# Reordering loads, conversions and gate operations at the start and in the second sweep of a hybrid GLA/MLA layer

## Chip, cores and metric

The kernel runs on one core of one Trainium2 chip, as one program. The time is the device time of one execution in microseconds; a smaller time is better. Times of several executions are given as their median.

## The reference

One layer of an encoder on 2048 tokens of width 1024, float32. The input projection feeds two groups of heads: gated linear attention (GLA) in chunks, forward and backward, with a low-rank gate; and multi-head latent attention (MLA) with rotary keys and a softmax over all keys. Both outputs pass one output projection, a residual and a layer norm.

```python
h = x @ w_in                      # columns: q k v gate lr_f lr_b | cq ckv kr gate
log_a = log_sigmoid(lr @ wg2 + bg) / 16            # decay, per direction
o_a = rms_norm(gla(q, k, v, log_a_fwd) + flip(gla(flip(q, k, v, log_a_bwd)))) * silu(gate)
q = rms_norm(cq) @ w_uq;  kv = rms_norm(ckv) @ w_ukv
o_b = softmax(q_nope k_nope^T + rope(q_rope) rope(k_rope)^T) v * silu(m_gate)
out = layer_norm(alpha * x + concat(o_a, o_b) @ w_out)
```

## The kernel before, in words

Float32 operands are split into a high part (a copy to fp32r, helper `hi`, line 367, mostly on ScalarE, ACT) and a low part (the difference, helper `lo`, line 373, on VectorE, DVE, or GpSimd, POOL). A product is then three matmuls, high by high, high by low and low by high (`mm3`, lines 421 to 423). Because helpers record these operations, the profile's lines are told apart by the names of the tiles. The 2048 tokens are 16 chunks of 128.

**First sweep** (`sweep_a`): step i handles chunk 15 - i. `products` multiplies the chunk's x (`xah`, `xal`) by the GLA weights `wA` in three groups of columns (288, 384, 384), eight products of 128 rows each, into PSUM tiles `ipa`. What a group yields is then taken out: `lr` (the low-rank gate input) and `q2` from group 0, `k2` and `v1` from group 1, `v3` from group 2. `ga_lrT` transposes lr (tile `lrT`) and copies it to `lrTs`; `ga_z` multiplies it with the gate weights `wg` (matmul z, line 891); three ACT functions, VectorE's running sums and so on follow. Before step 0 stands a prologue: the loads of x for chunk 15 (`xaf`), of 13 weight pieces (`was0` to `was2`, in `W_PIECES`), the identity, the gate weights `wgf` with a column `wgm`, and the next x; every piece is converted to `wah` and `wal` in a chained order (`in_order(worder)`). Loads are issued on SyncE's queue (SP). Steps 0 to 3 are interleaved by the list `ORDER_A`, which fixes the order on every engine; elsewhere a scheduler in the framework orders the instructions of each engine by their place in the program and by when their inputs are ready. A closed pool's space is reused tile by tile.

**Between the sweeps** (`late_gates`): the weights `wm` and `wz` of the second sweep are converted by `load_ws` from pools of 17 buffers for 8 raw pieces, 8 high and 8 low parts. The order of ACT and VectorE there is fixed by the lists `TAIL_ACT` and `TAIL_DVE`.

**Second sweep** (`sweep_c`): eight steps of two chunks. Each small operation has a name and a place: step number plus a number from `PLACE_C` (or `PLACE_C_FIRST` for step 0 and `PLACE_C_LAST` for step 7; the two numbers of a pair are for the even and the odd chunk). All operations are sorted by place and written in that order, chained on every engine:

```python
last = dict(self.tail)
for _, _, fn, a in sorted(todo, key=lambda e: e[:2]):
    with self.in_order(last):
        fn(*a)
```

The names that matter here: `xh`, `xl` are the high and low part of a chunk's x, in the tiles `xch` (ACT) and `xcl` (POOL), which hold one step's two chunks; `ipa` to `ipd` are the four quarters of the chunk's product with `wm` (tile `ipm`, line 1281, six matmuls each); `pz` 0 to 7 are the eighths of the step's product with `wz` (line 1210); `gm1` to `gm4` make the MLA gate from it (ACT, ACT, ACT, VectorE; lines 1215 to 1224); `qhb`, `qlb`, `MMh`, `MMl` prepare the operands of `Ob`, the output of the GLA state (lines 1438 and 1439); `oia`, `oib`, `rgd`, `og` turn that into the normed output (VectorE, og at line 1465); `krf` and `krfa` apply the rotary angles to the key (VectorE, then an addition on POOL, line 1315); `tm` transposes; `pq` is the absorbed query product. `Ob`, the gate product `pz` and `pq` share a PSUM pool `gp` of two buffers. In a step after the first, the matmuls of a chunk's quarters stand in this order, with x's low part as the third kind:

```python
order = [(p, k) for k in range(NK) for p in range(2)] + [(2, k) for k in range(NK)]
x = (self.xch, self.xch, self.xcl)[p]
```

So quarter `ipc` reads the first two pieces of `xcl` and `ipd` the other six. `pz` n reads all of both chunks' x of two of the eight pieces in step 7, pieces 2n and 2n + 1 for n up to 3. After the second sweep come the softmax attention and the output projection, which the change leaves alone.

Of the kernel before, what the change touches and what calls it, by code (L numbers as in the profile page):

```python
# [9 lines left out]
F32 = mybir.dt.float32  # L10
F32R = mybir.dt.float32r
I32 = mybir.dt.int32
AF = mybir.ActivationFunctionType
ALU = mybir.AluOpType
# [4 lines left out]
P = 128  # L19
S = 2048  # L20
D = 1024
NK = D // P
NCH = S // P
H = 4
# [116 lines left out]
    Ob=(0.141, 0.861),  # L141
# [50 lines left out]
    gm2=0.832,  # L192
# [66 lines left out]
    MMl=(-0.109, 0.558),  # L259
    krfa=(-0.119, 0.94),  # L260
    krsl=(0.252, 1.09),
# [9 lines left out]
    gm1=0.643,  # L271
    gm2=0.686,
    gm3=0.706,
    gm4=0.804,
    sgm=1.056,
# [10 lines left out]
    ipd=(0.042, 0.445),  # L286
    Ob=(-0.03, 0.299),
    tm=(0.495, 1.083),
# [30 lines left out]
    qrTl=(1.081, 2.186),  # L319
    xl=(-0.244, 0.038),  # L320
    M=(-0.531, -0.11),
# [35 lines left out]
class K:  # L357
# [100 lines left out]

    def load_ws(self, pool, srcs, ncols, tag, on_pool=()):


        names = lambda p: [f"{tag}{p}{k}" for k in range(NK)]
        raw = [pool.tile([P, ncols], F32, tag=tag, name=n) for n in names("r")]
        for r, src in zip(raw, srcs):
            self.w_load = self.nc.sync.dma_start(r, src).ins
        yield
        wh = [pool.tile([P, ncols], F32R, tag=tag, name=n) for n in names("h")]
        W = []
        for k, n in enumerate(names("l")):
            wl = pool.tile([P, ncols], F32R, tag=tag, name=n)  # L470
            self.hi(wh[k], raw[k])
            self.lo(wl, raw[k], wh[k], "pool" if k in on_pool else "dve")
            W.append((wh[k], wl))
        yield W

# [140 lines left out]
    def sweep_a(self):  # L616
        tc, nc, ins, cp = self.tc, self.nc, self.ins, self.cp
        with ExitStack() as ctx:
# [6 lines left out]
            rmask = wp.tile([P, H, P], F32, name="rmask")  # L625
            wgm = wp.tile([98, 1], F32, name="wgm")
            wg = wp.tile([98, H, P], F32R, name="wg")
# [17 lines left out]
            with tc.tile_pool(name="sta", bufs=1, reuse_waits="tile") as sta:  # L645
                xf = self.load_x(NCH - 1, "xa", 1, 2)
                xcur = self.split_x(xp, xf, NCH - 1, "xa", "dve", 2)
                wgf = sta.tile([98, H * P], F32, name="wgf")
                wgh = sta.tile([98, H * P], F32R, name="wgh")
                wdone, worder = [], {}  # L650
                for g, (c0, n) in enumerate(A_GROUPS):
                    k = 0
                    for m in W_PIECES[g]:
                        st = sta.tile([P, m, n], F32, name=f"was{g}_{k}")
                        nc.sync.dma_start(st, ins[f"wA{g}"][:, k:k + m])
                        ks, cs = slice(k, k + m), slice(c0, c0 + n)
                        with self.in_order(worder):
                            for e in [slice(j, j + 1) for j in range(m)] if g == 0 else [slice(0, m)]:
                                kh, kl = wah[:, ks, cs][:, e], wal[:, ks, cs][:, e]
                                ops = self.hi(kh, st[:, e]), self.lo(kl, st[:, e], kh)  # L660
                        k += m
                        wdone.append(ops)
                    if g == 1:
                        nc.sync.dma_start(self.ident, ins["ident"])
                        nc.sync.dma_start(wgf, ins["wg"])
                        nc.sync.dma_start(wgm, ins["wgm"])
                with self.in_order(worder):
                    self.hi(wgh, wgf)
                    nc.vector.scalar_tensor_tensor(wg.rearrange("p h d -> p (h d)"), wgh.bitcast(F32), wgm[:, 0:1],
                                                   wgf, ALU.mult, ALU.add)  # L670
                xnext = self.split_x(xp, self.load_x(NCH - 2, "xa", 1, 2), NCH - 2, "xa", "dve", 2)
                nc.sync.dma_start(rmask, ins["rmask"])
                nc.sync.dma_start(mask, ins["mask"])
# [8 lines left out]
            run = lambda n, i: [0 for _ in getattr(self, "ga_" + n)(ch[i])]  # L682
            ch[0]["x"], ch[1]["x"] = xcur, xnext

# [14 lines left out]
            self.first_lr = wdone[7][0]  # L699
            step(0, {(1, 7): [("lrT", "cur")]})  # L700
            run("bst", 0)
# [42 lines left out]
    def products(self, d, g, after=lambda g, k: None):  # L744
# [16 lines left out]
        if i == 0 or i > 3:  # L761
            for n in (("lr", "q2"), ("k2", "v1"), ("v3",))[g]:
                for _ in getattr(self, "ga_" + n)(d):
                    pass
# [303 lines left out]
    def late_gates(self):  # L1068
# [7 lines left out]
        self.wabs_l = bc.tile([P, 2, H, P], F32R, name="wabs_l")  # L1076
        wm = self.load_ws(self.wm, [ins["wB"][k, :, 512:960] for k in range(NK)], 448, "wm")
        wz = self.load_ws(self.wz, [ins["wB"][k, :, 960:1472] for k in range(NK)], 512, "wz")
        next(wm)
# [887 lines left out]
def layouts(inputs):  # L1967
# [19 lines left out]
    wg, bg = wg.reshape(32, H * P), bg.reshape(1, H * P)  # L1987
    a["wg"] = np.concatenate([wg, wg, wg, bg, bg], axis=0)
    wgm = np.zeros((98, 1), np.float32)
    wgm[64:96] = -1.0  # L1990
    wgm[97] = -1.0
    a["wgm"] = wgm
    a["gn_col"] = g["gla_norm_g"][0].reshape(P, 1)
# [41 lines left out]
```

## Time and profile before

| | us |
|---|---|
| median of 3 executions | 1308.29 (1307.52 to 1310.21) |
| the profiled execution | 1306.76 |
| its span, first to last instruction | 1304.7 |
| TensorE busy | 1284.8 (98%) |
| VectorE, ScalarE, GpSimd busy | 961.9, 817.2, 785.9 |

The first sweep with its prologue takes the first 360 us or so of the span, the second sweep runs to about 612, the attention and the output projection fill the rest. In the page's chain of work that ended last, TensorE has 91%. A row of the timeline gives start and duration in us, engine, line, operation, output tile, input tiles, shapes and, in brackets, how long the engine sat idle before it and what ended that. Ends of matmuls are modelled; the distance between two starts is the better measure of their rate.

### The profile page before, as it was taken

The numbers are of one execution on the slowest core, as the hardware profiler recorded it, in microseconds if no ns is written. First come the engines' busy times: TensorE is split into PE (matmuls) and PEld (weight loads), VectorE is DVE, ScalarE is ACT, GpSimd is POOL, SyncE is SP. The second block draws the span as 40 slices with busy tenths as digits, with TensorE's granted clock in tenths as the row PEclk, the third lists the DMA queues.
The fourth block names the chain that finished last, engine by engine and source line by source line (L and its number), as shares of the span: only waits on it lengthen the run. The fifth ranks groups of instructions, "written<-read, shape, count | busy, mean of one in ns | idle before, by whom it ended". The sixth has DMA issues, their size and how long they took to land.

```text
span 1304.7 us, 19969 instructions
## 1 busy us (share of the span) xinstructions
PE 1284.8 (98%) x7082; PEld 1131.1 (87%) x7082; DVE 961.9 (74%) x1706; ACT 817.2 (63%) x1334; POOL 785.9 (60%) x494
## 2 busy tenths in 40 slices
PE   7999999999999999999999999999999999999997
PEld 7999999999999999999788888888888887888886
DVE  6966675656675555555888888888888888469997
ACT  6765655566676566564778787878888888511110
POOL 0143333242467667661488888889999999844441
PEclk9999999999999999999999999999999999999999
DMA  8132313131475555656301111121123210366662
GB/s 285 62 101 54 94 53 94 49 88 59 155 247 194 187 178 200 207 176 209 90 1 41 41 42 41 41 62 60 57 71 101 47 41 9 121 203 202 214 196 97
DMA packets 105908, 145.81 MB, mean 112 GB/s; under 512 B 16743, under 2 KB 59375, under 8 KB 105809
## 3 DMA queue, kind: packets, MB, share of 16 engines
q1 hardware_dynamic: 97744, 142.41, 34.8%
q0 software_dynamic: 672, 2.10, 0.4%
q8 instruction: 56, 0.92, 0.3%
q10 hardware_dynamic: 7392, 0.03, 0.3%
q14 instruction: 44, 0.35, 0.1%
HBM read 94.14 MB, written 50.36 MB: 111 GB/s over the span
## 4 chain that ended last, share of the span: by engine, by line
PE 91%; DVE 2%; ACT 2%; issue 1%; POOL 0%; SPq 0%; DMA 0%; DVEq 0%; ACTq 0%
PE pz L1210 7%; PE ipm L1281 5%; PE o L421 5%; PE o L423 5%; PE o L422 5%; PE pS L1541 4%; PE pS L1544 4%; PE pS L1543 4%; PE pS L1545 4%; PE pS L1542 4%; PE ipa L421 4%; PE ipa L422 4%; PE ipa L423 4%; PE po L421 2%; PE po L423 2%; PE po L422 2%
## 5 line engine op out<-in xcount | busy, mean ns | idle before, releaser
L373 POOL TENSOR_TENSOR pl<-s,ph 128x1024 fp32r<-128x1024 f32 x128 | 307.0, 2413 | 67.0 <-ACT ph L367 61.7
L1563 DVE TENSOR_TENSOR rm<-pS,rm 128x512 f32<-128x512 f32 x210 | 144.9, 690 | 44.7 <-ACT s L1550 39.6
L1550 ACT ACTIVATE s<-pS 128x1024 f32<-128x1024 f32 x128 | 131.4, 1027 | 68.2 <-PE pS L1545 66.2
L1587 DVE TENSOR_TENSOR s<-s,mb 128x1024 f32<-128x1024 f32 x128 | 151.2, 1213 | 9.1 <-PE mb L1581 9.0
L1039 POOL TENSOR_TENSOR Us<-Us,cw 128x512 f32<-128x512 f32 x16 | 20.0, 1248 | 228.5 <-DVE Us L1037 190.0
L367 ACT ACTIVATE ph<-s 128x1024 fp32r<-128x1024 f32 x128 | 135.0, 1056 | 18.3 <-PE o L423 17.8
L1591 ACT ACTIVATE s<-s 128x1024 f32<-128x1024 f32 x128 | 131.4, 1050 | 13.4 <-DVE s L1587 13.4
L421 PE MATMUL ipa<-wah,xah 128*128 128x384 f32 (+1 forms) x384 | 130.0, 339 | 6.5 <-ACT wah L367 6.4
L422 PE MATMUL ipa<-wal,xah 128*128 128x384 f32 (+1 forms) x384 | 125.7, 327 | 0.0
L423 PE MATMUL ipa<-wah,xal 128*128 128x384 f32 (+1 forms) x384 | 125.2, 326 | 0.0
L1541 PE MATMUL pS<-qh,ckvT_h 128*128 128x512 f32 x256 | 103.7, 405 | 0.7 <-ACT s L1591 0.4
L421 PE MATMUL o<-ph,vh 128*128 128x512 f32 x256 | 102.6, 401 | 0.0
L423 PE MATMUL o<-ph,vl 128*128 128x512 f32 x256 | 101.3, 396 | 0.0
L1544 PE MATMUL pS<-rh,krs 128*128 128x512 f32 x256 | 101.2, 395 | 0.0
L422 PE MATMUL o<-pl,vh 128*128 128x512 f32 x256 | 101.1, 395 | 0.0
L1543 PE MATMUL pS<-qh,ckvT_l 128*128 128x512 f32 x256 | 100.9, 394 | 0.0
L1545 PE MATMUL pS<-rl,krs 128*128 128x512 f32 x256 | 100.7, 393 | 0.0
L1542 PE MATMUL pS<-ql,ckvT_h 128*128 128x512 f32 x256 | 100.6, 393 | 0.0
L1614 DVE TENSOR_TENSOR ap<-ap,s 128x512 f32<-128x512 f32 x120 | 83.1, 693 | 2.7 <-ACT s L1591 0.8
L373 POOL TENSOR_TENSOR ol<-of,oh 128x512 fp32r<-128x512 f32 x32 | 43.0, 1345 | 64.7 <-ACT oh L367 64.7
L421 PEld LDWEIGHTS ipa<-wah,xah 128*128 128x128 f32 x384 | 73.4, 191 | 7.6 <-ACT wah L367 6.8
L422 PEld LDWEIGHTS ipa<-wal,xah 128*128 128x128 f32 x384 | 73.5, 191 | 0.9 <-DVE wal L373 0.4
(325 smaller groups left out, 3839.4 us busy)
## 6 DMA issues: line engine op xcount, KB each, us to landing
xcf<-xT_dram SPq DMA_DIRECT2D x16, 512.0 KB, 5.4
xr<-x_dram SPq DMA_DIRECT2D x16, 512.0 KB, 5.3
out_dram<-rr SPq DMA_DIRECT2D x32, 256.0 KB, 2.0
xaf<-xT_dram SPq DMA_DIRECT2D x14, 512.0 KB, 4.3
oib<-oi_s SPq DMA_DIRECT2D x16, 256.0 KB, 4.0
qdb<-qd_s SPq DMA_DIRECT2D x16, 256.0 KB, 4.2
SU<-su_s SPq DMA_DIRECT2D x16, 256.0 KB, 4.4
ub<-u_s SPq DMA_DIRECT2D x16, 256.0 KB, 4.6
```

The lines of the kernel that those rows point to most:

```text
L367: return nc.scalar.activation(dst, src, AF.Copy).ins
L373: return e.tensor_tensor(dst, src, hi.bitcast(F32), ALU.subtract).ins
L421: mm(out, ah, bh, start=start, stop=False)
L422: mm(out, ah, bl, start=False, stop=False)
L423: mm(out, al, bh, start=False, stop=stop)
L1541: mm(ps[:, e], kh, qh, start=True, stop=False)
L1542: mm(ps[:, e], kh, ql, start=False, stop=False)
L1543: mm(ps[:, e], kl, qh, start=False, stop=False)
L1544: mm(ps[:, e], kr, rh, start=False, stop=False)
L1545: mm(ps[:, e], kr, rl, start=False, stop=True)
L1563: V.tensor_tensor(d["rm"], src[:, e], d["rm"], ALU.max)
L1587: V.tensor_tensor(s, s, d["mb"][:, None, :].to_broadcast([P, 2, QB]), ALU.subtract)
```

## The change

It has these parts. In the prologue, x of chunk 15 is loaded and converted in two halves, the second behind two weight pieces; the gate weights come behind all weight pieces instead of behind group 1, with `wgm` as their last column instead of a load of its own; the next x is split behind step 0 instead of ahead of it. In step 0, `lrT` follows product 5 of group 1 instead of its end, and `q2` follows group 1 instead of group 0. In `load_ws`, the high parts of all eight pieces are written ahead of the low parts (`high_first`), for `wm` and `wz`. In the second sweep's step 0, `gm2` to `gm4` move behind `xh` of chunk 2 (0.81), with og of chunk 0 (0.804) now ahead of gm4, and `krfa` of chunk 0 moves behind `MMl`, `qlb` and `Sf2`. In step 7, `Ob` of chunk 14 moves from 6.97 to 7.0, behind `ipc` of that chunk (6.996); `xl` of chunk 15 moves from 7.038 to 7.64, behind `krfa` of chunk 15 (7.636).

```diff
--- before.py
+++ after.py
@@ -257,7 +257,7 @@
     Sf2=(-0.613, -0.022),
     qlb=(-0.023, 0.63),
     MMl=(-0.109, 0.558),
-    krfa=(-0.119, 0.94),
+    krfa=(-0.02, 0.94),
     krsl=(0.252, 1.09),
     vl=(0.627, 1.365),
     qrfa=(1.04, 1.476),
@@ -269,9 +269,9 @@
     soT=(1.342, 1.538),
     pz=(-0.249, -0.195, -0.111, -0.018, 0.405, 0.452, 0.485, 0.622),
     gm1=0.643,
-    gm2=0.686,
-    gm3=0.706,
-    gm4=0.804,
+    gm2=0.815,
+    gm3=0.82,
+    gm4=0.83,
     sgm=1.056,
     pq=1.431,
     qah=1.57,
@@ -284,7 +284,7 @@
     ipb=(-0.04, 0.303),
     ipc=(-0.004, 0.42),
     ipd=(0.042, 0.445),
-    Ob=(-0.03, 0.299),
+    Ob=(0.0, 0.299),
     tm=(0.495, 1.083),
     pqr=(0.749, 1.284),
     tq=(0.919, 2.161),
@@ -317,7 +317,7 @@
     ckvTl=(0.88, 1.703),
     qrf=(0.795, 1.556),
     qrTl=(1.081, 2.186),
-    xl=(-0.244, 0.038),
+    xl=(-0.244, 0.64),
     M=(-0.531, -0.11),
     Sf1=(-0.688, -1.423),
     Sf2=(-0.624, 1.82),
@@ -456,7 +456,7 @@
         self.lo(wl, st, wh, lo_eng)
         return wh, wl
 
-    def load_ws(self, pool, srcs, ncols, tag, on_pool=()):
+    def load_ws(self, pool, srcs, ncols, tag, on_pool=(), high_first=False):
 
 
         names = lambda p: [f"{tag}{p}{k}" for k in range(NK)]
@@ -466,9 +466,13 @@
         yield
         wh = [pool.tile([P, ncols], F32R, tag=tag, name=n) for n in names("h")]
         W = []
+        if high_first:
+            for h, r in zip(wh, raw):
+                self.hi(h, r)
         for k, n in enumerate(names("l")):
             wl = pool.tile([P, ncols], F32R, tag=tag, name=n)
-            self.hi(wh[k], raw[k])
+            if not high_first:
+                self.hi(wh[k], raw[k])
             self.lo(wl, raw[k], wh[k], "pool" if k in on_pool else "dve")
             W.append((wh[k], wl))
         yield W
@@ -623,7 +627,6 @@
             wah, wal = (wp.tile([P, NK, NA], F32R, name=f"wa{p}") for p in "hl")
             mask = wp.tile([P, P], I32, name="mask")
             rmask = wp.tile([P, H, P], F32, name="rmask")
-            wgm = wp.tile([98, 1], F32, name="wgm")
             wg = wp.tile([98, H, P], F32R, name="wg")
             lrs = [wp.tile([P, 98], F32R, name=f"lr{i}") for i in range(2)]
             qbh = [wp.tile([P, H, 2, P], F32R, name=f"qbh{i}") for i in range(1)]
@@ -643,14 +646,20 @@
             nc.vector.memset(Sb, 0.0)
 
             with tc.tile_pool(name="sta", bufs=1, reuse_waits="tile") as sta:
-                xf = self.load_x(NCH - 1, "xa", 1, 2)
-                xcur = self.split_x(xp, xf, NCH - 1, "xa", "dve", 2)
-                wgf = sta.tile([98, H * P], F32, name="wgf")
+                xf = self.xfp.tile([P, NK, P], F32, tag="xf", name=f"xaf{NCH - 1}", bufs=2)
+                xcur = [xp.tile([P, NK, 1, P], F32R, tag=f"x{p}", name=f"xa{p}{NCH - 1}", bufs=2) for p in "hl"]
+                wgf = sta.tile([98, H * P + 1], F32, name="wgf")
                 wgh = sta.tile([98, H * P], F32R, name="wgh")
                 wdone, worder = [], {}
                 for g, (c0, n) in enumerate(A_GROUPS):
                     k = 0
                     for m in W_PIECES[g]:
+                        if g == 0 and k in (0, NK // 2):
+                            xs = slice(k, k + NK // 2)
+                            nc.sync.dma_start(xf[:, xs], ins["xT"][NCH - 1][:, xs])
+                            with self.in_order(worder):
+                                self.hi(xcur[0][:, xs, 0], xf[:, xs])
+                                self.lo(xcur[1][:, xs, 0], xf[:, xs], xcur[0][:, xs, 0])
                         st = sta.tile([P, m, n], F32, name=f"was{g}_{k}")
                         nc.sync.dma_start(st, ins[f"wA{g}"][:, k:k + m])
                         ks, cs = slice(k, k + m), slice(c0, c0 + n)
@@ -662,13 +671,12 @@
                         wdone.append(ops)
                     if g == 1:
                         nc.sync.dma_start(self.ident, ins["ident"])
-                        nc.sync.dma_start(wgf, ins["wg"])
-                        nc.sync.dma_start(wgm, ins["wgm"])
+                nc.sync.dma_start(wgf, ins["wg"])
                 with self.in_order(worder):
-                    self.hi(wgh, wgf)
-                    nc.vector.scalar_tensor_tensor(wg.rearrange("p h d -> p (h d)"), wgh.bitcast(F32), wgm[:, 0:1],
-                                                   wgf, ALU.mult, ALU.add)
-                xnext = self.split_x(xp, self.load_x(NCH - 2, "xa", 1, 2), NCH - 2, "xa", "dve", 2)
+                    self.hi(wgh, wgf[:, :H * P])
+                    nc.vector.scalar_tensor_tensor(wg.rearrange("p h d -> p (h d)"), wgh.bitcast(F32),
+                                                   wgf[:, H * P:], wgf[:, :H * P], ALU.mult, ALU.add)
+                xnext = self.load_x(NCH - 2, "xa", 1, 2)
                 nc.sync.dma_start(rmask, ins["rmask"])
                 nc.sync.dma_start(mask, ins["mask"])
             nc.sync.dma_start(pos_i, ins["pos"])
@@ -680,7 +688,7 @@
             ch = self.ch = [dict(cst, c=NCH - 1 - i, i=i, lr=lrs[i % 2]) for i in range(NCH)]
             self.wa = [(wah[:, k], wal[:, k]) for k in range(NK)]
             run = lambda n, i: [0 for _ in getattr(self, "ga_" + n)(ch[i])]
-            ch[0]["x"], ch[1]["x"] = xcur, xnext
+            ch[0]["x"] = xcur
 
             def step(i, steps):
 
@@ -697,7 +705,8 @@
                     self.gate_end(ch[i]["c"], g1)
 
             self.first_lr = wdone[7][0]
-            step(0, {(1, 7): [("lrT", "cur")]})
+            step(0, {(1, 5): [("lrT", "cur")]})
+            ch[1]["x"] = self.split_x(xp, xnext, NCH - 2, "xa", "dve", 2)
             run("bst", 0)
             self.wgr = [self.wgp.tile([P, 512], F32, tag="wg", name=f"wgr{k}") for k in range(NK)]
             for k, raw in enumerate(self.wgr):
@@ -759,7 +768,7 @@
                 after(g, k)
             yield k
         if i == 0 or i > 3:
-            for n in (("lr", "q2"), ("k2", "v1"), ("v3",))[g]:
+            for n in ((("lr", "q2"), ("k2", "v1"), ("v3",)) if i else (("lr",), ("q2", "k2", "v1"), ("v3",)))[g]:
                 for _ in getattr(self, "ga_" + n)(d):
                     pass
 
@@ -1074,8 +1083,8 @@
         self.wqr_l = bc.tile([P, 2, 256], F32R, name="wqr_l")
         self.wabs_h = bc.tile([P, 2, H, P], F32R, name="wabs_h")
         self.wabs_l = bc.tile([P, 2, H, P], F32R, name="wabs_l")
-        wm = self.load_ws(self.wm, [ins["wB"][k, :, 512:960] for k in range(NK)], 448, "wm")
-        wz = self.load_ws(self.wz, [ins["wB"][k, :, 960:1472] for k in range(NK)], 512, "wz")
+        wm = self.load_ws(self.wm, [ins["wB"][k, :, 512:960] for k in range(NK)], 448, "wm", high_first=True)
+        wz = self.load_ws(self.wz, [ins["wB"][k, :, 960:1472] for k in range(NK)], 512, "wz", high_first=True)
         next(wm)
         next(wz)
         xc = self.load_x(0, "xc")
 ...
-    a["wg"] = np.concatenate([wg, wg, wg, bg, bg], axis=0)
+    wg = np.concatenate([wg, wg, wg, bg, bg], axis=0)
 ...
-    a["wgm"] = wgm
+    a["wg"] = np.concatenate([wg, wgm], axis=1)
```

## The prediction

> **What bounds the kernel now.** I read the page first, then TensorE's waits, then the timeline around each of them.
>
> ```profile
> PE 1284.8 (98%) x7082; PEld 1131.1 (87%) x7082; DVE 961.9 (74%) x1706; ACT 817.2 (63%) x1334; POOL 785.9 (60%) x494
> ```
>
> The span is 1304.7 us, so TensorE idles for 19.9 us, and that is all a change of order can win. Part of it is the tail behind the last matmul. The waits view of TensorE holds the rest; these are the rows that the change can reach (total, times, longest):
>
> ```profile
> PE ipa L421 <- ACT wah L367: 6.4, 2, 6.0
> PE z L891 <- ACT lrTs L367: 0.7, 1, 0.7
> PE Ob L1439 <- POOL qlb L373: 0.6, 1, 0.6
> PE Ob L1438 <- POOL MMb L373: 0.4, 1, 0.4
> PE Ob L1438 <- DVE gm L1224: 0.3, 1, 0.3
> ```
>
> They lie in three places: the start (6.4 + 0.7), step 0 of the second sweep (0.3) and its step 7 (0.6 + 0.4). Between them TensorE runs nearly without a gap, so what is won or lost in one place mostly reaches the end.
>
> **The start.** Timeline; the columns are start, duration, engine, line, operation:
>
> ```profile
> 4.64 0.63 ACT L367 ACTIVATE xah<-xaf 128x512 fp32r<-128x512 f32 x1 [0.31 <-DMA xaf<-xT_dram]
> 5.46 0.78 ACT L367 ACTIVATE wah<-was 128x288 fp32r<-128x288 f32 x2 [0.19 <-DMA was<-wA_dram]
> 5.96 0.61 PE L421 MATMUL ipa<-wah,xah 128*128 128x288 f32 x1 [5.96 <-ACT wah L367]
> 7.99 2.23 ACT L367 ACTIVATE wah<-was 128x288 fp32r<-128x288 f32 x6 [1.74 <-DMA was<-wA_dram]
> 15.92 3.66 ACT L367 ACTIVATE wah<-was 128x768 fp32r<-128x768 f32 x5 [0.92 <-DMA was<-wA_dram]
> 16.80 3.89 DVE L373 TENSOR_TENSOR wal<-was,wah 128x768 fp32r<-128x768 f32 x5 [0.88 <-ACT wah L367]
> 17.83 0.42 PE L422 MATMUL ipa<-wal,xah 128*128 128x384 f32 x1
> 20.01 1.14 ACT L367 ACTIVATE xah<-xaf 128x512 fp32r<-128x512 f32 x2
> 20.60 0.74 DVE L669 SCALAR_TENSOR_TENSOR wg<-wgh,wgm,wgf 98x512 fp32r<-98x512 f32 x1
> 21.38 0.60 ACT L367 ACTIVATE q<-ipa 128x512 f32<-128x512 f32 x1 [0.24 <-DVE wg L669]
> 22.51 0.29 ACT L367 ACTIVATE lrTs<-lrT 98x128 fp32r<-98x128 f32 x1
> 22.85 0.66 PE L891 MATMUL z<-lrTs,wg 98*128 98x128 f32 x4 [0.74 <-ACT lrTs L367]
> 23.73 0.38 PE L421 MATMUL ipa<-wah,xah 128*128 128x288 f32 x1
> ```
>
> With the second half of x behind two weight pieces, the first piece lands earlier by the spacing of such transfers, 5.46 - 4.64 = 0.82, and the first matmul comes at about 5.15. But products 4 to 7 need the same bytes as before (all of x and three pieces), so this helps only as far as the later chain moves too.
>
> It does move. The third column group is tied to the conversion of its weights: the low part of its first piece (two products wide, so about a quarter of 3.89) ends near 17.7, and the matmul that reads it starts at 17.83. That conversion waited for its transfer (0.92 idle). Moving the gate weights behind all pieces and dropping wgm takes 196 KB from ahead of it: 0.58 at the 338 GB/s of this window (last column), 0.5 to 0.7 in round numbers.
>
> ```profile
> 15.00:20.00 5.00, 5.00 (x30) 4.88 (x29) 4.05 (x6) 3.79 (x6) 0.00 (x0) 1.00 0.98 338
> ```
>
> So step 0's products end some 0.6 earlier. Then comes z. Its input lrTs was copied last but one in ACT's queue (22.51), behind q and k; its transposition is now issued after product 5 of group 1 and the copy stands ahead of both, so the 0.74 goes. It can't go below wg, though: q waited for wg at 21.38, which I read as step 0's first tile lying where wgf lay, and after the change the first tile is lrTs. With wg done at 20.7, lrTs, q and k follow (0.3 + 0.6 + 0.6), k's transposition starts near 22.3, and step 1's products near 22.8 instead of 23.73: a gain of 0.9.
>
> Two things take from it. The split of step 1's x (1.14 on ACT, then VectorE) is now traced behind step 0. If ACT does it while it would wait for wg, it is free; if it stands behind v3, the third matmul of step 1 waits until about 22.3 + 0.6 + 0.7 = 23.6 (half of ACT's 1.14, and a VectorE operation as long as wg's), and only 0.1 to 0.4 is left. And later TensorE waits for VectorE, whose chain starts with z's functions on ACT; these come earlier by less than TensorE does, so part of the gain turns into more of this wait:
>
> ```profile
> 53.83 0.33 PE L1032 MATMUL Up<-VV,ktl 128*128 128x128 f32 x1 [0.46 <-DVE ktl L373]
> ```
>
> I take **-0.5**, with the ends -1.2 (all of 0.9 and some of the earlier first matmul) and +0.5 (next part). The other loads on SP's queue (x of step 1, the masks, positions) move up by one transfer; nobody waits for them.
>
> **The slow stretch.** The first matmuls are slow, though the granted clock reads 1.00 in the window above:
>
> ```profile
> 12.74 0.45 PE L422 MATMUL ipa<-wal,xah 128*128 128x288 f32 x1
> 12.98 0.45 PE L423 MATMUL ipa<-wah,xal 128*128 128x288 f32 x1
> 17.20 0.34 PE L422 MATMUL ipa<-wal,xah 128*128 128x384 f32 x1
> 17.37 0.34 PE L423 MATMUL ipa<-wah,xal 128*128 128x384 f32 x1
> ```
>
> The spacing is 0.24 for 288 columns early and 0.17 for 384 later; at the early rate 384 would take 0.32. TensorE had then run without a real gap since 7.99 + 0.4 = 8.4. After the change, products 0 to 3 end near 5.15 + 12 x 0.24 = 8.0, and product 4's weights, the third of six conversions, are ready near 7.99 + 3 x 0.37 = 9.1. The gapless run thus starts 0.7 later. If the speed-up comes that much later, seven matmuls of 0.15 more, 1.0, are lost: the start's -0.5 becomes +0.5. The Trainium skill's page "TensorE: Matmul & The Clock Gate" (Part 1: The HAM clock gate) speaks against this change in that way: it says that full clock comes after one busy window of about 3.4 us, whose phase does not depend on the kernel's start. The rows agree in that the fast rate follows a gapless run.
>
> **Weights, high parts first.** Between the sweeps ACT's conversions waited for VectorE's:
>
> ```profile
> 372.89 0.63 ACT L367 ACTIVATE wzh<-wzr 128x512 fp32r<-128x512 f32 x1 [0.62 <-DVE wzl L373]
> ```
>
> A high part that waits for another piece's low part means that buffers go to whoever asks first, and low parts had taken them. With the high parts first this wait goes from ACT. TensorE waits for neither there, and VectorE is the slower of the two: 0, between -0.3 and +0.3 (half the wait, for another order of the neighbours).
>
> **Step 0 of the second sweep.** Ob of chunk 1 needs one of two PSUM buffers: one holds step 0's gate product until gm4 (L1224) has read it, the other chunk 0's Ob until og (L1465) has.
>
> ```profile
> 394.23 1.23 DVE L1224 TENSOR_TENSOR gm<-pz,gm 128x1024 f32<-128x1024 f32 x1 [3.85 <-ACT gm L1221]
> 394.05 1.04 ACT L367 ACTIVATE xch<-xcf 128x1024 fp32r<-128x1024 f32 x1
> 395.37 1.12 DVE L1465 SCALAR_TENSOR_TENSOR og<-Ob,rg_r,ub 128x128 f32<-128x128 f32 x4
> ```
>
> VectorE had nothing to do from 390.4 (3.85 before gm4): og stood behind gm4 in its queue. Now og goes first and frees its buffer near 391.5, well before 395.5, where Ob got one. gm2 and gm3 stand behind xh's 1.04, so gm4 ends at 396.5; behind it VectorE's next work waits for Ob anyway. **-0.3.** krfa of chunk 0 moves behind three POOL operations; cq and ckv, behind its reader on ACT, come later but still ahead of TensorE's tm: 0, at most +0.5.
>
> **Step 7** cuts both ways.
>
> ```profile
> 576.42 1.28 POOL L373 TENSOR_TENSOR qlb<-qdb,qhb 128x512 fp32r<-128x512 f32 x1 [0.17 <-ACT qhb L367]
> 576.83 0.28 PE L1438 MATMUL Ob<-MMb,qhb 128*128 128x256 f32 x1
> 577.75 0.33 PE L1439 MATMUL Ob<-MMb,qlb 128*128 128x128 f32 x1 [0.64 <-POOL qlb L373]
> 578.34 2.41 POOL L373 TENSOR_TENSOR xcl<-xcf,xch 128x1024 fp32r<-128x1024 f32 x1
> 583.56 0.39 PE L1438 MATMUL Ob<-MMb,qhb 128*128 128x256 f32 x1 [0.42 <-POOL MMb L373]
> 587.14 1.22 PE ipm L1281 x6
> 578.80 0.69 DVE L1442 TENSOR_TENSOR oib<-Ob,oib 128x512 f32<-128x512 f32 x1 [0.26 <-PE Ob L1439]
> 586.45 1.13 DVE L1465 SCALAR_TENSOR_TENSOR og<-Ob,rg_r,ub 128x128 f32<-128x128 f32 x4
> 588.19 0.28 PE L421 MATMUL pq<-cqT_h,wabs_h 128*128 128x256 f32 x1
> ```
>
> Ob of chunk 14 now follows six more products (1.22, the chain of waits has such a group), so it starts at 578.05, when qlb is done: 0.64 goes. Without xl of chunk 15 (2.41) in POOL's queue, chunk 15's qlb and MMl are ready in time: 0.42 goes. But chunk 14's Ob ends 0.3 to 0.4 later than now. VectorE waited for it at 578.80 and works back to back from there to og's end at 587.58, so og ends near 587.9; og frees the buffer that pq needs, and TensorE would be there at 588.19 - 1.06 = 587.1. Some 0.8 of the 1.06 comes back as a wait of pq: **-0.25** is left, between -1.06 and 0.
>
> Then xl itself. At 7.64 it stands behind ipc and ipd of chunk 15 (7.42, 7.445) and pz 0 and 1 of step 7 (7.572, 7.578), which read that tile. They now read the low part that chunk 13 left there and wait for nothing; the write must wait for the last of them, and pz 2 must wait for the write.
>
> ```profile
> 595.50 0.28 PE L1210 MATMUL pz<-xcl,wzh 128*128 128x256 f32 x1
> 595.86 0.28 PE L1210 MATMUL pz<-xcl,wzh 128*128 128x256 f32 x1
> ```
>
> The first row is pz 1's last reader, the second pz 2's first. TensorE's order is chained, so nothing passes. The reads end at 595.78; a hand-over takes 0.05 (qlb ends at 577.70, its reader starts at 577.75); then 2.41 and a hand-over back: 598.29 instead of 595.86, **+2.4**. POOL's operations behind xl wait for VectorE's work that comes later still.
>
> **Sum:** -0.5 - 0.3 - 0.25 + 2.4 = +1.4 (rounded up from 1.35). The profiled execution took 1306.8 in all, its span and 2.1 around it; so 1308.2. The median of the runs shown, 1308.3, lies 1.5 above it: **1309.7**.
>
> **Rivals.**
> 1. PSUM buffers are handed out in turn. Then Ob of chunk 1 waits for gm4 in any case, which ends 1.04 later: +1.0 instead of -0.3, the sum +2.7, 1311.0: slower. It decides as soon as gm4 ends after 395.2. For it: Ob did wait for gm4. Against: ACT's wait for wzl, which buffers in turn would not make. 0.12.
> 2. The start gains nothing (longer slow stretch, or x's split behind v3): 0 to +0.5, the sum +1.9 to +2.4, about 1310.4. For it: the later gapless run. Against: transfers, not TensorE, set the third group. 0.25, of it 0.13 for the slow stretch.
> 3. The last low part costs nothing, because the placement numbers don't order it as I read them: the sum -1.0, 1307.3. Against: the list is sorted by these numbers, and each engine is chained along it. 0.13.
>
> My forecast has 0.50.
>
> **How the numbers follow.** 0.2% is 2.6 us, about what a measurement of this kernel can tell from no change. Slower: most of rival 1 (0.09), a quarter of rival 2, whose upper end and 1 us between medians reach 2.6 (0.07), and 0.07 of the forecast's own for an order of the first sweep that I can't see: 0.23. Faster: half of rival 3, with the start's full gain, 0.07. The rest, 0.70, is within. The range goes from rival 3 (0.4 below it for the start) at 1306.9 to rival 1 with half a microsecond less at the start, 1311.6.
>
> **What would show it.** First matmul at 5.1 to 5.3; z without a wait; og near 391 and no wait of Ob for gm; one wait of pz for POOL's xcl of 2.3 to 2.5; pq waiting for og, under 1 us. If pz has no such wait, the forecast is wrong by 2.4; if Ob waits over 1 us for gm, by 1.3; if z still waits, the start is wrong.

## The result

| kernel | median, us | the kernel before on the same chip | ratio (95% interval) |
|---|---|---|---|
| changed | 1313.05 (1305.66 to 1315.52) | 1308.35 | 1.0035 (1.0018 to 1.0051) |
| changed, timed again with the last experiments | 1312.64 (1309.91 to 1316.24) | 1307.37 | 1.0041 (1.0029 to 1.0053) |

The change makes the kernel about 5 us slower. Forecast was 1309.7 with a range up to 1311.6, so 1.4 slower: the sign was right, the size was not. One of the six executions of the first row took 1305.66, at a mean granted clock of 0.999 where the other five show 0.995 to 0.998; no trace of it was kept, so what it was spared isn't known. The profiled execution of the changed kernel took 1313.46, its span is 1311.4, against 1306.76 and 1304.7.

From the page, the first part (engine, busy us and share of the span):

```profile
PE 1287.7 (98%) x7082; PEld 1132.7 (86%) x7082; DVE 967.1 (74%) x1706; ACT 816.7 (62%) x1334; POOL 788.3 (60%) x494
```

TensorE's idle time grew from 19.9 to 23.7 us. But the span grew by 6.7: TensorE was also busy for 2.9 us longer with the same 7082 matmuls, so some of them ran slower. VectorE, too, was busy 5.2 longer with the same operations. TensorE's waits (total, times, longest):

```profile
PE ipa L421 <- ACT wah L367: 5.4, 1, 5.4
PE pz L1219 <- DVE wzl L373: 2.7, 2, 1.7
PE pz L1219 <- POOL xcl L373: 2.2, 1, 2.2
PE pqr L421 <- ACT oT L1484: 0.8, 1, 0.8
PE z L900 <- ACT lrTs L367: 0.2, 1, 0.2
```

The three rows of Ob are gone, z's wait is 0.2 instead of 0.7, and the wait for xcl is there with 2.2 where 2.4 was forecast. The second row is new, and nothing in the prediction has it: the first gate product, pz of step 0, waits for the low parts of its weights.

Here it is in TensorE's timeline (the two matmuls that waited, two behind them, and two of the later ones):

```profile
378.77 0.39 PE L1219 MATMUL pz<-xch,wzl 128*128 128x256 f32 x1 [1.66 <-DVE wzl L373]
380.46 0.58 PE L1219 MATMUL pz<-xch,wzl 128*128 128x256 f32 x1 [1.05 <-DVE wzl L373]
...
383.12 0.41 PE L1219 MATMUL pz<-xcl,wzh 128*128 128x256 f32 x1
383.33 0.41 PE L1219 MATMUL pz<-xch,wzl 128*128 128x256 f32 x1
...
384.06 0.28 PE L1219 MATMUL pz<-xch,wzh 128*128 128x256 f32 x1
384.18 0.28 PE L1219 MATMUL pz<-xcl,wzh 128*128 128x256 f32 x1
```

Two things are to be seen: two pauses of 2.7 together, and behind them a spacing of 0.21 between starts, where 0.12 is normal. The table by windows says why (length, busy time of PE, PEld, DVE, ACT and POOL with their counts, granted clock, DMA share, GB/s); first the changed kernel, then the kernel before, its second window alone:

```profile
376.00:380.00 4.00, 1.75 (x13) 1.33 (x11) 3.91 (x2) 0.00 (x0) 3.85 (x3) 1.00 0.01 5
380.00:384.00 4.00, 3.54 (x16) 3.48 (x17) 3.15 (x11) 1.51 (x7) 1.32 (x2) 0.57 0.30 89
```

```profile
380.00:384.00 4.00, 4.00 (x33) 3.90 (x32) 2.13 (x9) 3.60 (x13) 3.92 (x4) 1.00 0.82 232
```

The granted clock is 0.57 behind the pause; in the kernel before it is 1.00. The trace records the half clock from 380.49 for 3.41 us, and again from 602.36, behind the wait for xcl, also for 3.41.

Why are the low parts late? VectorE's row for the eight subtractions, the longest of them by itself, and POOL's rows beside it, changed kernel:

```profile
369.15 12.04 DVE L373 TENSOR_TENSOR wzl<-wzr,wzh 128x512 fp32r<-128x512 f32 x8
374.89 3.83 DVE L373 TENSOR_TENSOR wzl<-wzr,wzh 128x512 fp32r<-128x512 f32 x1
374.33 1.37 POOL L1416 TENSOR_TENSOR Sf<-Sf,cw 64x512 f32<-64x512 f32 x1
375.66 1.29 POOL L373 TENSOR_TENSOR MMb<-SU,MMb 128x512 fp32r<-128x512 f32 x1
376.92 1.25 POOL L373 TENSOR_TENSOR qlb<-qdb,qhb 128x512 fp32r<-128x512 f32 x1
378.13 1.72 POOL L1419 TENSOR_TENSOR Sf<-Sf,SU 64x512 f32<-64x512 f32 x1
382.19 0.32 POOL L1324 TENSOR_TENSOR krf<-krf,rope 128x64 f32<-128x64 f32 x1 [2.34 <-DVE rope L1499]
```

and the kernel before:

```profile
371.58 5.99 DVE L373 TENSOR_TENSOR wzl<-wzr,wzh 128x512 fp32r<-128x512 f32 x8
375.20 1.81 POOL L1410 TENSOR_TENSOR Sf<-Sf,SU 64x512 f32<-64x512 f32 x1 [5.23 <-DMA SU<-su_s]
377.10 1.37 POOL L1415 TENSOR_TENSOR SU<-Sf,cw 64x512 f32<-64x512 f32 x1
378.54 1.04 POOL L1407 TENSOR_TENSOR Sf<-Sf,cw 64x512 f32<-64x512 f32 x1
379.54 0.32 POOL L1315 TENSOR_TENSOR krf<-krf,rope 128x64 f32<-128x64 f32 x1
379.83 1.29 POOL L373 TENSOR_TENSOR MMb<-SU,MMb 128x512 fp32r<-128x512 f32 x1
```

The eight began 2.4 earlier and ended 3.6 later, in 12.04 us instead of 5.99. By tile, minimum, median and longest of one in ns, kernel before and changed kernel:

```profile
L373 DVE TENSOR_TENSOR wzl<-wzr,wzh x8: 673/679/1603, 371.6 to 376.0; 128x512 fp32r<-128x512 f32 x8
```

```profile
L373 DVE TENSOR_TENSOR wzl<-wzr,wzh x8: 693/1140/3830, 369.1 to 380.5; 128x512 fp32r<-128x512 f32 x8
```

The one slow subtraction of the kernel before (1603) is the last, the only one that starts while a POOL operation is at work. (The one ahead of it had started 0.01 before POOL's operation at 375.20 and kept its time; there POOL's operation is the longer one, 1.81 where the changed kernel has 1.28 for it.) In the changed kernel POOL is at work from 371.52 to 379.85 with no pause over 0.08, and one subtraction takes 3.83: it starts during the product at 374.33 and ends at 378.72, 0.55 behind the end of qlb. The theory that follows: a VectorE operation with two operands in SBUF can't run while a POOL operation does; it gets its turn when POOL pauses between two. The Trainium skill's page "GPSIMD Engine Reference" (1. Specifications) says that GpSimd's SBUF interfaces are shared with VectorE, and that VectorE instructions with two SBUF inputs contend for them; it gives no price.

### The profile page after: what moved, and what is told of

Same layout as the page of the kernel before. It is cut to its first block, busy times and chain, and to the rows that moved or that the text cites. A ratio compares the mean times of both kernels' runs of the same rounds, so it can differ in the third digit from the quotient of the medians.

```text
span 1311.4 us, 19958 instructions
## 1 busy us (share of the span) xinstructions
PE 1287.7 (98%) x7082; PEld 1132.7 (86%) x7082; DVE 967.1 (74%) x1706; ACT 816.7 (62%) x1334; POOL 788.3 (60%) x494
## 4 chain that ended last, share of the span: by engine, by line
PE 91%; DVE 2%; ACT 1%; DMA 1%; issue 1%; POOL 0%; SPq 0%; DVEq 0%; ACTq 0%
PE pz L1219 7%; PE ipm L1290 6%; PE o L421 5%; PE o L423 4%; PE o L422 4%; PE pS L1550 4%; PE pS L1553 4%; PE pS L1552 4%; PE pS L1554 4%; PE pS L1551 4%; PE ipa L421 4%; PE ipa L422 4%; PE ipa L423 4%; PE po L421 2%; PE po L423 2%; PE po L422 2%
## 5 line engine op out<-in xcount | busy, mean ns | idle before, releaser
L1219 PE MATMUL pz<-xch,wzl 128*128 128x256 f32 x256 | 72.9, 288 | 2.7 <-DVE wzl L373 2.7
```

The lines of the kernel that those rows point to most:

```text
L1219: self.nc.tensor.matmul(s["pz"][:, h], self.Wz[k][w][:, h * P:(h + 1) * P], x2(x, k), start=(k == 0 and p == 0), stop=stop.get(h) == (k, p))
```

## The experiments

All medians are to be read against the kernel before, timed beside them: 1307.16 for the first four, 1307.20 for the next four, 1307.37 for the last four.

**The low part back early** (changed kernel, one number):

```
-    xl=(-0.244, 0.64),
+    xl=(-0.244, 0.038),
```

> The changed kernel with the last x's low part back at 0.038; everything else as changed. Theory: this edit costs the wait of pz 2 (2.2 us) and, behind it, a window of 3.4 us at half the granted clock (about 1.7 us); Ob of chunk 15 gets a wait of some 0.4 for POOL's MMb back. So the median falls by 3.5, from 1313.0 to about 1309.5, pz has no wait for xcl, and the clock reads 1.00 between 590 and 620 us. Rival: only the wait counts, the half clock is covered by later idle time: 1311.2. Both: the waits of pz for wzl near 378 stay.

1311.22, ratio 1.0025 (1.0015 to 1.0036). No wait for xcl, one half clock only (near 381), and Ob has a wait of 1.1 for MMb. By the ratios that is 1.3 to 2.1 below the changed kernel, where 3.5 was expected, so the rival's figure is the nearer one here; the last comparison has the edit's price again, with both kernels timed side by side. What is left of the loss is in the weights.

**The weights' old order** (changed kernel):

```
-wm = self.load_ws(..., 448, "wm", high_first=True)
-wz = self.load_ws(..., 512, "wz", high_first=True)
+wm = self.load_ws(..., 448, "wm")
+wz = self.load_ws(..., 512, "wz")
```

> The changed kernel with the old order of the weights' conversions (each high part followed by its low part); the rest as changed. Theory: high parts first lets ACT run ahead, which brings the loads of SU and with them POOL's chain forward by more than the start alone does, into VectorE's eight wzl subtractions; without it POOL's first addition to Sf comes near 373.5, about two wzl operations meet it, their mean is at most 1.0 us instead of 1.5, pz waits for wzl under 0.8 us instead of 2.7, no half clock near 380, and the median falls by about 4 to 1309. Rival: the earlier start alone makes them meet: pz still waits 2 to 3 us and the median stays within 1 us of 1313.

1309.49, ratio 1.0015 (1.0006 to 1.0024). pz has no wait for wzl. Three subtractions met POOL, not two, with 1.52 to 1.77 each (mean of the eight 1.03), but they ended in time. By the ratios the kernel is 2.6 to 3.4 below the changed one, where 4 was expected. POOL's chain ran no further into them, since MMb waited for its high part from ACT:

```profile
379.17 1.29 POOL L373 TENSOR_TENSOR MMb<-SU,MMb 128x512 fp32r<-128x512 f32 x1 [2.70 <-ACT MMb L367]
```

**Both back** (the two diffs above together):

> The changed kernel with both of these edits taken back: the new start, the gate operations of step 0, krfa and Ob of chunk 14 remain. Theory: no pause of TensorE above 1 us is left behind the start, no half clock; the start gives 1.6, step 0 0.3, chunk 14's Ob about 0.3: 1306.2, that is 2 below the kernel before. Rival: the start's 1.6 was the luck of where the full clock began in that one execution, and is 0.5 on the average: 1307.3.

1306.41, ratio 0.9990 (0.9980 to 1.0000), no half clock. That is 0.75 below the kernel before by the medians and 1.3 by the ratio, nearer to the rival's 1 than to the 2 expected. So with these two edits taken back there is no loss left; each costs on top of it 4.8 (1311.22 - 1306.41) and 3.1 (1309.49 - 1306.41). Both are more than the waits that they make, which brings up the clock.

**TensorE kept at work through the pause** (the weights' old order, late low part; `zw` is a tile of zeros):

```
+        if last and n == 2:
+            for _ in range(20):
+                matmul(s["pz"][:, 0], self.zw, x2(self.xch, 0), start=False, stop=False)
```

> As the kernel with the old order of the weights' conversions and the late low part, but with 20 further matmuls that add zero weights to pz ahead of pz 2 (20 x 0.12 = 2.4 us), so that TensorE works where it waited for the low part. Theory (the half clock is caused by the pause): the span between pz 1 and pz 2 stays as long (2.2 to 2.4 us), but the clock stays at 1.00 behind it, and the median lies 1 to 1.7 below that kernel. Rival (the half clock has another cause): it is there as before, and the median is the same or up to 0.2 above.

1307.93, ratio 1.0002 (0.9993 to 1.0011): 1.56 faster than the same kernel without the 20 matmuls. The matmuls take the place of the pause:

```profile
593.58 2.53 PE L1221 MATMUL pz<-xch,zw 128*128 128x256 f32 x20
```

The windows behind the pause, first without them and then with them:

```profile
598.00:602.00 4.00, 4.00 (x23) 4.00 (x22) 1.57 (x8) 0.00 (x0) 0.80 (x2) 0.57 0.02 4
```

```profile
598.00:602.00 4.00, 4.00 (x36) 4.00 (x35) 1.57 (x8) 1.07 (x3) 1.42 (x3) 1.00 0.03 8
```

With useless work in the pause, 36 matmuls instead of 23 run in the four microseconds behind it: the half clock is the pause's doing. 3.41 us at half rate is 1.7 of work; 1.56 came back.

**SU's loads later** (changed kernel with the low part early):

```
-    u15=-0.21,
+    u15=-1.125,
```

> The changed kernel with the low part early (0.038), the weights' high parts first as changed, and one more edit: the store of the first ub (u15) is placed ahead of the loads of SU in SP's queue (-1.125 instead of -0.21), so that these go out near 369.7 instead of 366.3 and POOL's first addition to Sf starts near 374 instead of 371. Theory (VectorE's subtractions of two SBUF operands wait for POOL's operation under way): six or seven of the eight wzl now run alone at 0.69, pz has no wait for wzl above 0.5, no half clock near 380; the median is that of the kernel without high parts first, 1306.4 (0.75 below the kernel before), against 1311.2 with the early loads. Rival (high parts first slow the low parts or hand the buffers over in a worse order by itself): pz still waits about 3 us for wzl and the median stays near 1311.

1309.52, ratio 1.0016 (1.0005 to 1.0027): about 1.2 better than the first experiment by the ratios, where 4.8 was expected. A miss. Its POOL rows and its row by tile:

```profile
375.88 1.37 POOL L1416 TENSOR_TENSOR Sf<-Sf,cw 64x512 f32<-64x512 f32 x1
377.21 1.26 POOL L373 TENSOR_TENSOR MMb<-SU,MMb 128x512 fp32r<-128x512 f32 x1
378.44 1.25 POOL L373 TENSOR_TENSOR qlb<-qdb,qhb 128x512 fp32r<-128x512 f32 x1
379.66 1.72 POOL L1419 TENSOR_TENSOR Sf<-Sf,SU 64x512 f32<-64x512 f32 x1
```

```profile
L373 DVE TENSOR_TENSOR wzl<-wzr,wzh x8: 691/810/3807, 369.2 to 376.4; 128x512 fp32r<-128x512 f32 x8
```

POOL's first addition moved from 371.0 in the first experiment to 373.0 (near 374 was expected), one subtraction fewer met it, but the last one again took 3.8 and pz waited 2.5 for it. So a later start of POOL's chain, by this much, doesn't help. The long subtraction starts at 376.44, during the product of Sf, and ends 3.81 later, 0.56 behind the end of qlb: product, MMb and qlb follow each other without a gap (377.21 + 1.26 is already past 378.44), and VectorE got no turn between them. Between the operations ahead of these there is a gap of about 0.08, and there it comes in. Behind qlb it came in without a gap, and the addition to Sf took 1.72 instead of some 1.29; why there and not earlier, the runs don't show. What let MMb and qlb run into wzl at all is the question that this left.

**POOL kept busy in the kernel before:**

```
-        self.nc.gpsimd.tensor_tensor(self.Sf, d["Sf"], ...)
+        for _ in range(9 if d["c"] == 0 else 1):
+            self.nc.gpsimd.tensor_tensor(self.Sf, d["Sf"], ...)
```

> The kernel before, with POOL's first product of Sf (1.03 us at 368.9) done nine times instead of once, the result being the same: POOL is busy from 369 to about 378.5, where it was idle from 370 to 375.2. Theory: each wzl that meets it ends 0.55 after a POOL operation, 1.4 us or more instead of 0.68, so the eight end at 382 or later instead of 377.6; pz waits 3 to 5 us for wzl and the clock is halved for a window behind it: 4.5 to 6.5 us slower than the kernel before. Rival (the slow subtractions have nothing to do with POOL): wzl keeps 0.68 and the time is that of the kernel before, at most 0.5 more for the later chain on POOL.

1312.44, ratio 1.0041 (1.0029 to 1.0054): 5.2 slower. VectorE's eight subtractions by tile, and POOL's eight extra products:

```profile
L373 DVE TENSOR_TENSOR wzl<-wzr,wzh x8: 925/1522/1526, 370.7 to 380.4; 128x512 fp32r<-128x512 f32 x8
```

```profile
369.17 12.03 POOL L1408 TENSOR_TENSOR Sf<-Sf,cw 64x512 f32<-64x512 f32 x8
```

Nothing but POOL's load was changed, and a subtraction takes 1522 ns instead of 679. POOL pays too: 1.50 (12.03 / 8) from one product to the next, some 0.08 of it a gap, where one product took 1.03. The two take turns. pz waited 2.5 for wzl (less than the 3 to 5 expected), Ob another 0.8 for the late qlb, and a half clock followed.

**The low part in between** (the weights' old order):

```
-    xl=(-0.244, 0.64),
+    xl=(-0.244, 0.2),
```

> The changed kernel with the weights' old order, and with the last x's low part at 0.2: behind POOL's low parts of chunk 15's q and state (0.166, 0.195), yet ahead of its first reader (ipc, 0.42), so that it neither delays Ob of chunk 15 nor has to wait for readers. Theory: Ob's wait of 1.05 for MMb goes, xcl is written by 582, five us ahead of its reader, no other wait appears: 1305.4, that is 1.0 below the kernel with the low part at 0.038 and 1.8 below the kernel before. Rival: VectorE's chain behind Ob (oib, og, oT) is the bound there, and the 1.05 comes back as a longer wait of pqr for oT: 1306.4.

1306.00, ratio 0.9991 (0.9982 to 1.0000). Ob's wait of 1.05 is gone; pqr's wait for oT rose from 0.8 to 1.0. A wait of 0.5 of Ob for qlb stands in step 0, which the expectation did not have. The median is 0.4 below that of the kernel with 0.038, from two comparisons with the kernel before, which doesn't tell the two expectations apart.

**The start alone** (the kernel before with the edits of the first sweep and nothing else):

> The kernel before with the new start alone (x in two halves among the weight pieces, gate weights behind them, wgm in wg, group 1 and the split of step 1's x reordered). Theory: the full clock begins up to one window of 3.4 us earlier or later by chance, so single executions mislead; on the average the start gives 0.5 to 1.0: 1306.3 to 1306.7 against 1307.2. Rival (the 1.6 of the profiled execution is the start's real worth): 1305.6. Second rival (the start gives nothing, and the gain of the kernel with both edits back comes from step 0 and chunk 14's Ob): 1307.2.

1306.04, ratio 0.9992 (0.9983 to 1.0001): 1.2 faster, with an interval that just reaches no change: between the 0.5 to 1.0 expected here and the first rival's 1.6, above the prediction's 0.5 and within its ends.

**krfa back** (changed kernel, one number):

```
-    krfa=(-0.02, 0.94),
+    krfa=(-0.119, 0.94),
```

> The changed kernel with krfa of chunk 0 alone put back to -0.119 (it was -0.02), high parts first and the late low part as changed. Theory: krfa, which waits for VectorE's rope, stood ahead of MMl, qlb and the second addition to Sf in POOL's queue and kept these from running before VectorE was through with wzl; moved behind them, it lets the three run without a gap, and VectorE gets no turn for 3.8 us. With krfa back no wzl takes over 2 us, pz waits for wzl under 0.5 us, no half clock near 380, and the time is that of the kernel without high parts first: about 2.3 above the kernel before, 1309.5. Rival (high parts first is enough by itself to make the collision): pz keeps 2 to 3 us of waits and the time stays with the changed kernel's.

1309.30, ratio 1.0015 (1.0005 to 1.0025), against 1312.64 for the changed kernel beside it. pz has no wait for wzl. Its POOL rows and its row by tile:

```profile
375.82 1.37 POOL L1416 TENSOR_TENSOR Sf<-Sf,cw 64x512 f32<-64x512 f32 x1
378.74 0.32 POOL L1324 TENSOR_TENSOR krf<-krf,rope 128x64 f32<-128x64 f32 x1 [1.56 <-DVE rope L1499]
379.02 1.29 POOL L373 TENSOR_TENSOR MMb<-SU,MMb 128x512 fp32r<-128x512 f32 x1
```

```profile
L373 DVE TENSOR_TENSOR wzl<-wzr,wzh x8: 693/808/1584, 369.1 to 376.4; 128x512 fp32r<-128x512 f32 x8
```

POOL stops at krfa until VectorE's rope is done, and rope stands behind wzl in VectorE's queue. So krfa, an addition of 0.32 us that nobody seemed to need early, kept POOL's longest gapless stretch out of wzl: the last subtraction met the product of Sf alone. All that was expected of this run came.

**The changed kernel again, krfa back with the low part at 0.2, and high parts first alone**, all in one comparison with the kernel above:

> The changed kernel as it is, timed beside the ones that follow. If the prices of its two bad edits add up (4.8 and 3.1 us, from the kernels with one of them back) to the kernel with both back (0.75 below the kernel before), it lies 7.1 above the kernel before: 1314.3. If they share something (the half clocks, or the late low part hidden behind the first delay), 4.5 to 5.5 above: 1312.

> The changed kernel with krfa back at -0.119 and the last x's low part at 0.2; all else as changed, high parts first among it. Theory: start -1.1, Ob of step 0 -0.3, chunk 14's and 15's Ob -0.7: 1305.2 to 1306.0 where the kernel before has 1307.2. Rival: high parts first still costs some 1 to 2 us: 1307 to 1308.

> The kernel before with the weights' high parts first, and nothing else. Theory (the loss is high parts first together with krfa's move): POOL runs up to three operations into wzl, 0.85 each, then krfa holds it; pz waits for wzl under 0.3, and the time is within 0.5 of the kernel before: 1307.2. Rival (high parts first alone costs it): pz waits 2 us or more, 3 to 5 us slower: 1310 to 1312.

| kernel | median | ratio (95% interval) |
|---|---|---|
| changed | 1312.64 | 1.0041 (1.0029 to 1.0053) |
| changed, krfa at -0.119 | 1309.30 | 1.0015 (1.0005 to 1.0025) |
| the same, and the low part at 0.2 | 1306.49 | 0.9991 (0.9981 to 1.0000) |
| before, with high parts first alone | 1307.61 | 1.0002 (0.9991 to 1.0012) |

High parts first costs nothing by itself (+0.2): its longest subtraction takes 1.74, and pz doesn't wait. The first three rows are a chain: krfa's move 3.3, the late low part 2.8, all the rest -0.9; the sum is the +5.3 of the changed kernel. The late low part is 0.64 against 0.2 here. The single prices from above (4.8 and 3.1) add up to more than that, so of the two figures expected for the changed kernel the smaller one, 1312, came out; what the two edits share isn't shown. A 2.2 us pause doesn't always bring a half clock: in the profiled execution of the changed kernel timed again, the second pause brought none. The kernel with krfa back and 0.2 came out between what was expected (1305.2 to 1306.0) and the rival (1307 to 1308).

The kernel with both edits back, the one with the low part at 0.2, and the one with krfa back and 0.2 are all 0.8 to 1.2 below the kernel before, with intervals that end at 1.0000. They are clearly better than the changed kernel; that they beat the kernel before is likely, not shown beyond doubt, and among the three there is no difference to be told.

## Why the prediction was right or wrong

1. **The start: right in sign, undersized.** Forecast -0.5, measured -1.2 alone (ratio 0.9983 to 1.0001). The first matmul came at 5.35 (forecast 5.15). z's wait fell to 0.2. What failed is the reasoning on the slow stretch: the gapless run did not begin later. The conversions of the first four products' weights now go without a gap (first row), and product 4 started at 8.56, not at 9.1, so TensorE runs nearly gapless from 5.35, and the fast rate begins earlier, not later; its spacing is 0.14 here, 0.24 at this time before:

```profile
4.86 1.52 ACT L367 ACTIVATE wah<-was 128x288 fp32r<-128x288 f32 x4 [0.19 <-DMA was<-wA_dram]
...
5.35 0.61 PE L421 MATMUL ipa<-wah,xah 128*128 128x288 f32 x1 [5.35 <-ACT wah L367]
...
8.56 0.35 PE L421 MATMUL ipa<-wah,xah 128*128 128x288 f32 x1
...
9.38 0.29 PE L421 MATMUL ipa<-wah,xah 128*128 128x288 f32 x1
9.52 0.30 PE L422 MATMUL ipa<-wal,xah 128*128 128x288 f32 x1
```

   In the eleven profiles with the new start the recorded full clock begins between 8.4 and 11.4; in three with the old one at 12.6, 13.5 and 14.0. So where it begins differs by up to 3 us between executions with the same start; how much of their time that moves, the runs don't show. The prediction's granted clock of 1.00 was read from a window (15 to 20) that doesn't hold its slow matmuls: they stand at 12.74 and 12.98, ahead of the trace's first record of the full clock at 13.48. Nor do its seven slower matmuls follow from 0.7 us, into which two of 0.32 fit.

2. **Weights, high parts first, at 0: right for the edit alone, and the error lay beside it.** The step that failed is the sentence on krfa: "krfa of chunk 0 moves behind three POOL operations; ... 0, at most +0.5". It asked who waits for krfa, and never who had been held back behind it. The three operations are MMl, qlb and Sf2. With krfa behind them, MMl (tile MMb) and qlb followed the product of Sf without a gap, and the 3.83 us subtraction lay across all three; Sf2 is the addition that came next. The price of meeting POOL stood in the trace of before (1603 against 679 ns), too, but the prediction took VectorE's durations as fixed. Measured: +3.3 for krfa's move, with high parts first around it. By the traces it is a wait of pz of 2.5 to 2.7 and, as an estimate, 1.7 for the half clock behind it, less a wait of 0.5 of Ob for qlb that the kernel with krfa back has and the changed kernel hasn't. With the old order of the weights the move does no harm that shows (the kernel with both edits back has it and is not slower than the kernel before): there ACT delivers MMh only at 378.5 to 379.1, and POOL waits for that instead. The kernel before with krfa's move alone was not run.

3. **Step 0: right in what moves, not measurable in time.** og came ahead of gm4 and Ob did not wait for gm:

```profile
393.50 1.13 DVE L1474 SCALAR_TENSOR_TENSOR og<-Ob,rg_r,ub 128x128 f32<-128x128 f32 x4
398.12 1.23 DVE L1233 TENSOR_TENSOR gm<-pz,gm 128x1024 f32<-128x1024 f32 x1 [3.50 <-issue]
398.22 0.28 PE L1447 MATMUL Ob<-MMb,qhb 128*128 128x256 f32 x1
```

   og is at 393.5 instead of the 391 forecast because the pause of pz and the half clock lie ahead of it (without them, in the kernel with both edits back, it is at 389.25). That kernel differs from the start alone by +0.4 by the medians and -0.3 by the ratios, within the noise of the two, so -0.3 for this is neither shown nor refuted. The first rival (buffers in turn) is out: Ob of chunk 1 started at 398.22, while gm4 still ran.

4. **Step 7, Ob of chunk 14: right amount by the waits, other waiter.** Both waits of Ob went, 1.06 in all, and 0.78 came back; no run times this edit alone. But pq did not wait for og; pqr waits for oT, two operations further down the same chain:

```profile
588.75 0.39 PE L421 MATMUL pqr<-wqr_h,cqT_h 128*128 128x256 f32 x1 [0.78 <-ACT oT L1484]
```

5. **The last low part: the mechanism as forecast, the price not whole.** POOL waited for pz 1's last reader, pz 2 for POOL, 2.24 against 2.4:

```profile
598.47 2.34 POOL L373 TENSOR_TENSOR xcl<-xcf,xch 128x1024 fp32r<-128x1024 f32 x1 [1.16 <-PE pz L1219]
600.86 0.39 PE L1219 MATMUL pz<-xcl,wzh 128*128 128x256 f32 x1 [2.24 <-POOL xcl L373]
603.48 0.41 PE L1219 MATMUL pz<-xch,wzh 128*128 128x256 f32 x1
603.70 0.41 PE L1219 MATMUL pz<-xcl,wzh 128*128 128x256 f32 x1
```

   The last two rows are the part that was missed: 0.22 from one start to the next. With the half clock behind it the edit costs 2.8 in the last comparison (against 0.2), and 3.1 in the earlier one (against 0.038).

So the sum had the low part (+2.4 forecast, 2.8 measured) and the start (-0.5, -1.2), whose errors nearly cancel; the 3.3 of krfa's move were not in it at all, and they are what put the result outside the range. No rival held them either: each had one edit in view, and this loss needs two.

## What to carry to other kernels

When an operation is moved in an in-order queue, ask what had been waiting behind it: a small operation that waits may be the one that keeps its followers out of the way. Before making two engines overlap that did not, look for one operation in the trace that already met the other engine, and use that duration. And price a pause of the matmul engine of about 2 us or more with up to half a clock window on top of it.

## What the runs showed of the hardware

**VectorE and POOL take turns on operations with two SBUF operands.** A 128x512 subtraction on VectorE takes 0.68 alone and 1.52 when it meets one POOL operation after another with 0.08 between them; it takes 3.8 where it meets three POOL operations that follow without a gap, and ends about 0.55 behind the third. It goes the other way, too: POOL's first product of Sf took 3.47 in the changed kernel, where VectorE ran two xcl subtractions back to back, instead of 1.03. VectorE operations of the same size with one operand in PSUM show nothing of it: in the attention POOL is busy nearly all the time, and this group of the kernel before, which reads pS from PSUM, keeps 690 ns:

```profile
L1563 DVE TENSOR_TENSOR rm<-pS,rm 128x512 f32<-128x512 f32 x210 | 144.9, 690 | 44.7 <-ACT s L1550 39.6
```

**A pause shorter than a clock window can halve the clock.** The records of the granted clock change on a grid of 3.41 us that runs through the whole execution: in the changed kernel the two half clocks, at 380.49 and 602.36, lie 65 windows apart. Over the fourteen profiles, from the first full clock to the last matmul, seven of the eight windows in which TensorE idled for 1.6 us or more (the modelled ends of the matmuls taken) were followed by one window at half clock; no window with up to 1.44 idle was. The eighth, in the changed kernel timed again, had 1.78 idle, more than one that was followed by it (1.64), so these figures give no sharp limit. A pause of 2.47, in the kernel with SU's loads later, brought none: it lay across two windows, with about 1.2 in each. The Trainium skill's page "TensorE: Matmul & The Clock Gate" has the free-running window of about 3.4 us (What's actually happening), and these runs agree. Its rule to avoid pauses of over about 3 us (Why this matters for your kernels) is too generous here: pauses of 2.2 were enough, but for that one, when they fell mostly into one window.
